# Each query's sum of squares behind its own convolution, and held output rows through the common raw places

## The chip, the cores and the metric

The kernel runs on one core of a Trainium2 chip. Its engines work side by side: TensorE multiplies matrices (PE in the rows below; its weight loads are listed as PEld), VectorE (DVE) and ScalarE (ACT) work element by element, GpSimd (POOL) does small steps, and SyncE (SP) issues most of the DMA transfers. Each engine takes its own instructions in order; between engines, semaphores hold an instruction back until what it reads is there, or until the memory that it writes is free. The metric is the time of the core in microseconds (us) of device time, less is better. The time before is the median of three runs.

## The reference, cut to what matters

`reference` runs a first block (a state-space layer, feed-forward parts, an attention with shared keys and values) and then a second block of two layers on x, 256 positions by 1024 features, in float32. A layer of the second block is a feed-forward part, a hybrid mixer and another feed-forward part. The change is in the hybrid mixer:

```python
hcat = x @ w_in
qa, ka, va, qkv_b, beta_raw, dt_raw, z, gate_raw = jnp.split(hcat, SPLIT_POINTS, axis=-1)
ya = sliding_window_attention(qa, ka, va, pos_bias, sink) @ w_branch_a
qkv_b = jax.nn.silu(causal_depthwise_conv(qkv_b, conv_w))
qb, kb, vb = jnp.split(qkv_b, (QK_B, 2 * QK_B), axis=-1)          # 8 heads of 128
qb, kb = l2norm(qb), l2norm(kb)                                   # t * rsqrt(sum(t * t) + eps)
o = gated_delta_rule(qb, kb, vb, g, beta)                         # chunks of 128 positions
yb = (norm(o) * dn_norm_g * silu(z)) @ w_branch_b
return (gate_a * ya + gate_b * yb) @ w_out
```

The sums of squares of `l2norm` and the last product, that with `w_out`, are what the two edits touch.

## The kernel before, in words

**Weights.** All weights come from DRAM in units of 128 rows by 1024 columns (512 KB). `unit` (L158) takes a raw place, issues the load on SyncE (L161), and splits the values into a high part `wh`, a cast on ScalarE (L150), and a low part `wl`, a subtract on VectorE (L154, for convolutions halved between VectorE and GpSimd). Every product is made of three matmuls: high by high, high by low, low by high. There are three common raw places (WR = 3). SyncE works its queue in order: a load that waits for a place holds back all behind it.

**The mixer's program.** `weave` (L65) writes TensorE's order down when the program is built: tasks in lanes (one delta-rule head each, the preparation of a half, attention windows) are stepped when a model clock says that their inputs are due, and between them stands fill work, which is the list of weight products: z, the decay inputs, the convolutions of heads 0 to 3 and of heads 4 to 7 (keys, then queries, then values, `conv_half`, L1174), the attention projections, z again, the gates, and branch a. `yield hop()` in a task means that it comes back a fixed modelled time later; `yield "name"` means that it waits until fill or another task has put the name into `c.done`. The other engines' instructions are ordered by a scheduler. Branch b (the product with `w_branch_b`) follows the woven part, and behind it comes `w_out`.

**The sums of squares.** `conv` (L1144) computes one head's queries, keys or values: 24 matmuls, a scaled copy on ScalarE, three taps on VectorE, a Tanh, and a last product on VectorE into `kq[m]`, which holds query and key of head m. The preparation of a half, `prep(f)` (L1306), waits for the name `kq{f}`, set when all four queries of the half are there; squares them on ScalarE (line L1314, in four instructions), and adds the squares up with the small matrices `sel` on TensorE into one bank, a row per head. Behind that come a logarithm, the running sum of the decays, a row write by SyncE into DRAM, and loads of these rows by GpSimd, then chunk matrices (one set per head, called `keep2` products of queries and keys, with VectorE masks behind them) and a solve of the small diagonal blocks on GpSimd, whose result is loaded as `T16` and first used in `head` (L1413).

**The end of a head.** ScalarE squares the head's output (L1517), GpSimd makes the inverse root (L1518, L1519), VectorE multiplies (a line of `stt`), TensorE transposes and the result is split. Branch b needs it from all eight heads.

**The held rows.** `row_gemm` (L288) runs the product with `w_out`, eight units of 128 rows. The first three are multiplied as they come. The last five (MH = 5) are loaded and split into a pool of their own and are then gone through four times by `last_rows` (L276), once for each quarter of the output, so that each quarter's layernorm can start early. `hold_pools` (L138) makes the pool, and, where a number of raw places is given (MR = 2), two raw places that only held units use. The first units of the feed-forward part that follows are loaded in the same time.

Of the kernel before, what the change touches and what calls it, by code (L numbers as in the profile page):

```python
# [11 lines left out]
AF = mybir.ActivationFunctionType  # L12
# [4 lines left out]
T = 256  # L17
# [476 lines left out]
TAIL = 3.9  # L494
LAG = 7
HOLD = 6
MH, MR = 5, 2
TS = 8
NC = T // TS
NG, GC, NP = 64, 16, 64  # L500
# [545 lines left out]
NHH = NH // 2  # L1046
# [21 lines left out]
def hybrid(c, i, hT, state, place):  # L1068

    nc, I = c.nc, c.I  # L1070
    V, S, G, PE = nc.vector, nc.scalar, nc.gpsimd, c.pe
# [7 lines left out]
    hop = lambda n=1: n * (HM2 if late else HM)  # L1079
    with ExitStack() as ctx:  # L1080
# [4 lines left out]
        def tile_(kind, *sh, part=P):  # L1085
            n = int(np.prod(sh))
            names = "abcd"[:len(sh)]
            t = pools[kind].tile([P, 512 if kind[-1] == "2" else 256], F32, name=kind)[:part, :n]
            return t.rearrange(f"p ({' '.join(names)}) -> p {' '.join(names)}", **dict(zip(names, sh)))

        k2 = lambda *sh, part=P: tile_("k2", *sh, part=part)
# [11 lines left out]
        sel, cut, msk, lev, bd = c.mixer_consts  # L1103
# [13 lines left out]
        kq, bv, LA, zs, qa, ka, ca, gb, oT, kf, T16, vT = ({} for _ in range(12))  # L1117
# [26 lines left out]
        def conv(f, n, m):  # L1144

            src = n * NH + m
            w = c.unit(W("qkv")[src], SH_C)
            p = c.ps(T)
            yield from c.cols_steps(p, w, hx)
            a = k1(T)  # L1150
            S.activation(out=a, in_=p, func=AF.Copy, scale=cw[:, 3, src:src + 1])
            for d in (1, 2, 3):
                stt(a[:, d:], p[:, :T - d], cw[:, 3 - d, src:src + 1], a[:, d:], ALU.mult, ALU.add)
            h = k1(T)
            c.act(out=h, in_=a, func=AF.Tanh, scale=0.5)
            if n == 2:
                stt(h, h, 1.0, a, ALU.add, ALU.mult)
                return h
            if n == 1:
                kq[m] = keep2(2, T)  # L1160
            stt(kq[m][:, 1 - n], h, 1.0, a, ALU.add, ALU.mult)

        def v_flip(m):
            yield f"vT{m}"
# [9 lines left out]
        def conv_half(f):  # L1174
            heads = range(f * NHH, f * NHH + NHH)
            for n in (1, 0):
                for m in heads:
                    yield from conv(f, n, m)
            c.done.add(f"kq{f}")
            if f == 0:  # L1180
                beta_cols()
            for m in heads:
                vT[m] = yield from conv(f, 2, m)
                c.done.add(f"vT{m}")
# [120 lines left out]

        def prep(f):  # L1306

            yield f"kq{f}"

            pss = c.ps(2, T)  # L1310
            sq = []
            for h in range(NHH):
                sq.append(k2(2, T))
                S.activation(out=sq[h], in_=kq[f * NHH + h], func=AF.Square)  # L1314
            yield hop()
            for h in range(NHH):
                PE.matmul(pss[:NHH], lhsT=sel[:, h, :], rhs=sq[h], start=h == 0, stop=h == NHH - 1)
                yield 0.4
            lr = k2(2, T, part=NHH)
            V.tensor_scalar(out=lr, in0=pss[:NHH], scalar1=4e-6, scalar2=None, op0=ALU.add)  # L1320
            log = c.act(out=lr, in_=lr, func=AF.Ln)
# [39 lines left out]
            for h in range(NHH):  # L1361
                m = f * NHH + h
# [35 lines left out]
            for j in range(15):  # L1398
                n, w = 15 - j, j + 1
# [13 lines left out]
        def head(f, h):  # L1413
# [112 lines left out]
            for t in range(2):  # L1526
# [4 lines left out]

        weave(c,
              [[prep(0)] * (n == 0) + [head(m // NHH, m % NHH) for m in range(n, NH, LH)] for n in range(LH)] +
              [
               [v_flip(m) for m in range(NH)],
# [58 lines left out]
@with_exitstack  # L1594
def build(ctx, tc, I, O, stages):
    c = Core(ctx, tc, I, O)
    nc = tc.nc
    if MAN:
        ctx.enter_context(tc.manual_schedule(engines={mybir.EngineType.PE}))

    c.weight_pools(ctx, WR, WP - 1)
    hT = swish = None
    if "ssm" in stages:
        yT = c.pair(0)
        swish = Glu(c, yT)
        ssm(c, yT, [swish.ahead()])
    c.x = x = c.pool(ctx, "x", 1).tile([P, 2, D], F32, name="x")
    for t in range(2):
        nc.sync.dma_start(out=x[:, t], in_=I["x"][t * P:(t + 1) * P])
    c.hp.append(c.pool(ctx, "h1", 1))  # L1610
    second = "second" in stages or "mix" in stages or "sw" in stages
    if second:
        c.aside = mixer_inputs(c, c.pool(ctx, "mixc", 1))
        if "ffn0" not in stages:
            list(c.aside)


    plan = []
    for i in range(2):
        ffn = lambda j, i=i: ([I["ffn_w13_2_0"][i, j // 2, s] for s in range(2)], "ffn", i, j)  # L1620
        plan += [ffn(0), ([I["w_in_2_z"][i, n] for n in range(2)], "mix", i, 1), ffn(2)]
    plan = plan if "second" in stages else plan[1:3] if "mix" in stages else plan[:1] if "sw" in stages else []

    def ahead(n, hT):
        return c.ahead(hT, plan[n][0]) if n < len(plan) else ([], iter(()))

    with ExitStack() as cn:
        c.norm_pools(cn)
        c.taps = c.pool(cn, "taps", 1)
        hT, state = first_block(c, swish, stages, lambda hT: ahead(0, hT))  # L1630
        if hT is None:
            hT = c.pair(0)
            c.done = {"in0", "in1"}
            for t in range(2):
                c.flip(hT, x[:, t, :], t)
            state, go = ahead(0, hT)
            weave(c, [], [go], drain=True)
    place = 0

    for n, (_, kind, i, j) in enumerate(plan):  # L1640
        if kind == "mix":
            cT = hybrid(c, i, hT, state, 1 - place)
        else:
            place = 1 - place
        with ExitStack() as cn:
            if kind == "mix":
                c.spare_pool(cn)
                c.hold_pools(cn, MH, MR)
            c.norm_pools(cn)
            g, b = c.gains(I["ln_g_2"][i, j]), c.gains(I["ln_b_2"][i, j])  # L1650
            nc.gpsimd.tensor_scalar(out=x, in0=x, scalar1=ALPHA, scalar2=0.0, op0=ALU.mult, op1=ALU.add)
            ho = c.pair(place)
            next_state, go = ahead(n + 1, ho)

            def tail(t, acc):
                if t == 0:
                    c.done -= {"in0", "in1"}
                c.ln(t, acc, 0.5, g, b)
                if n + 1 == len(plan):
                    nc.sync.dma_start(out=O["out"][t * P:(t + 1) * P], in_=x[:, t])  # L1660
                    return
                yield from c.arrive(ho, x[:, t, :], t)

            if kind == "mix":
                weave(c, [], [c.row_gemm(I["w_out_2"][i], c.ktiles(cT), tail, MH), go], drain=True)
            else:
                c.ffn(hT, state, I["ffn_w13_2"][i, j // 2], I["ffn_w2_2"][i, j // 2], c.silu_gate, tail, [go])
        hT, state = ho, next_state
    if not plan:
        nc.sync.dma_start(out=O["out"].rearrange("(t p) d -> p t d", p=P), in_=x)  # L1670
# [218 lines left out]
```

## Time and profile before

| quantity | value |
|---|---|
| time, median of three runs | 2226.42 us (2223.49 to 2230.21) |
| profiled execution, its own time | 2223.28 us |
| span of the profiled execution | 2221.5 us |
| mean granted clock of TensorE | 0.982 of full speed |
| TensorE busy | 2135.0 us, 13908 matmuls |
| VectorE busy | 1537.0 us |
| ScalarE busy | 1182.5 us |
| GpSimd busy | 226.9 us |

The span goes from the first to the last instruction of the profiled execution. The busy shares are means over the whole program; where an engine stands still is read from the waits and the timelines. The two hybrid mixers lie at about 900 to 1280 us and 1650 to 2020 us.

### The profile page before, as it was taken

What the parts mean: (1) busy time and instruction counts of PE and PEld (TensorE: products, weight loads), DVE (VectorE), ACT (ScalarE), POOL (GpSimd) and SP (SyncE); (2) the same over time, 40 slices, a digit from 0 to 9 for tenths busy, and PEclk for the clock granted to TensorE, in tenths of its full rate; (3) what the DMA queues carried; (4) which work ended last, traced back from release to release, by engine and by line L of the source; (5) the groups of instructions that cost most, each with busy time, mean ns of one, the idle gap of its engine ahead of it and who ended that gap; (6) DMA issues with size and microseconds to landing.
All of it is one profiled execution on the core that took longest, in us unless ns stands there. A gap on an engine that the chain in (4) does not pass through costs nothing.

```text
span 2221.5 us, 36550 instructions
## 1 busy us (share of the span) xinstructions
PE 2135.0 (96%) x13908; PEld 1867.4 (84%) x13908; DVE 1537.0 (69%) x2615; ACT 1182.5 (53%) x2187; POOL 226.9 (10%) x360
## 2 busy tenths in 40 slices
PE   8889999999999999998999899999999899998998
PEld 7677888898888888897889788888889788997886
DVE  8855767576877666787755676676678876576665
ACT  4644656444655555465655355545546555544553
POOL 1001000000000000243400000000005242000000
PEclk9889999999999999999999999999999999999999
DMA  4325576543666565554434545555655453264663
GB/s 143 101 35 175 182 247 198 163 124 125 199 189 203 177 189 188 170 173 147 131 105 134 208 152 189 189 191 189 190 171 169 137 167 111 95 206 153 190 190 123
DMA packets 123471, 362.02 MB, mean 163 GB/s; under 512 B 24732, under 2 KB 38000, under 8 KB 123296
## 3 DMA queue, kind: packets, MB, share of 16 engines
q1 hardware_dynamic: 117696, 350.25, 50.4%
q0 software_dynamic: 5232, 9.37, 1.5%
q8 instruction: 110, 1.80, 0.3%
q14 instruction: 65, 0.53, 0.1%
q10 hardware_dynamic: 368, 0.07, 0.0%
HBM read 355.36 MB, written 5.04 MB: 162 GB/s over the span
## 4 chain that ended last, share of the span: by engine, by line
PE 74%; DVE 8%; DMA 7%; issue 4%; ACT 3%; POOL 1%; POOLq 0%; SPq 0%; DVEq 0%; ACTq 0%
PE ps L36 71%; PE ps L40 3%; DVE wl L154 3%; ACT wh L150 2%; DMA raw<-in_w_out_dram 2%; DMA raw<-in_ffn_w_dram 1%; DMA raw<-in_ffn_w_down_dram 1%; DMA raw<-in_w_in_z_dram 1%; DMA raw<-in_ssm_w_glu_dram 1%; DVE keep L1075 1%; DMA k<-scratch 1%; DVE prod L530 1%; POOL k L1074 0%; DVE k L1075 0%; DMA raw<-in_kv_w_v_dram 0%
## 5 line engine op out<-in xcount | busy, mean ns | idle before, releaser
L36 PE MATMUL ps<-xx,wh 128*128 128x256 f32 (+1 forms) x4064 | 1077.4, 340 | 4.6 <-DVE xx L154 2.6
L154 DVE TENSOR_TENSOR wl<-raw,wh 128x1024 fp32r<-128x1024 f32 (+1 forms) x614 | 738.1, 1204 | 332.5 <-ACT wh L150 322.7
L150 ACT CAST wh<-raw 128x1024 fp32r<-128x1024 f32 x614 | 643.6, 1050 | 324.7 <-PE ps L36 171.0
L36 PE MATMUL ps<-xx,wl 128*128 128x256 f32 x2992 | 803.4, 282 | 0.6 <-DVE wl L154 0.6
L36 PEld LDWEIGHTS ps<-xx,wh 128*128 128x128 f32 x4064 | 686.4, 191 | 91.9 <-issue 18.9
L36 PEld LDWEIGHTS ps<-xx,wl 128*128 128x128 f32 x2992 | 568.4, 190 | 22.0 <-DVE wl L154 0.8
L36 PE MATMUL ps<-wh,xx 128*128 128x256 f32 (+1 forms) x1152 | 258.3, 318 | 0.8 <-DVE xx L154 0.7
L225 ACT COPY sum<-ps 128x256 f32<-128x256 f32 x240 | 88.7, 371 | 251.7 <-PE ps L36 251.6
L36 PE MATMUL ps<-wl,gh 128*128 128x512 f32 x528 | 208.6, 395 | 0.0
L36 PE MATMUL ps<-wh,gl 128*128 128x512 f32 x528 | 207.9, 394 | 0.7 <-DVE gl L154 0.7
L36 PE MATMUL ps<-wl,xx 128*128 128x256 f32 (+1 forms) x576 | 189.7, 329 | 19.3 <-DVE wl L154 18.7
L36 PE MATMUL ps<-wh,gh 128*128 128x512 f32 x528 | 207.5, 393 | 0.0
L36 PEld LDWEIGHTS ps<-wh,xx 128*128 128x128 f32 x1152 | 193.5, 193 | 16.5 <-DVE xx L154 3.0
L226 DVE TENSOR_TENSOR sum<-ps,sum 128x256 f32<-128x256 f32 x240 | 101.2, 423 | 112.1 <-ACT sum L225 112.1
L36 PEld LDWEIGHTS ps<-wl,xx 128*128 128x128 f32 x576 | 111.0, 193 | 31.9 <-DVE wl L154 22.6
L36 PEld LDWEIGHTS ps<-wh,gl 128*128 128x128 f32 x528 | 99.0, 188 | 24.7 <-DVE gl L154 1.6
L36 PEld LDWEIGHTS ps<-wh,gh 128*128 128x128 f32 x528 | 99.2, 188 | 22.6
L36 PEld LDWEIGHTS ps<-wl,gh 128*128 128x128 f32 x528 | 99.2, 188 | 18.9 <-ACT gh L150 0.3
L332 POOL TENSOR_SCALAR v<-mv 128x1 f32<-128x1 f32 x12 | 7.3, 609 | 858.2 <-DVE mv L388 858.2
L150 ACT CAST xx<-ps 128x512 fp32r<-128x512 f32 (+1 forms) x64 | 31.8, 512 | 116.3 <-PE ps L40 115.8
L154 POOL TENSOR_TENSOR wl<-raw,wh 128x512 fp32r<-128x512 f32 x48 | 76.7, 1604 | 70.1 <-ACT wh L150 63.1
L1075 DVE SCALAR_TENSOR_TENSOR k<-ps,cw,k 128x255 f32<-128x255 f32 x144 | 68.5, 475 | 2.2
(291 smaller groups left out, 2315.3 us busy)
## 6 DMA issues: line engine op xcount, KB each, us to landing
raw<-in_ffn_w_dram SPq DMA_DIRECT2D x264, 512.0 KB, 3.6
raw<-in_ffn_w_up_dram SPq DMA_DIRECT2D x88, 512.0 KB, 4.2
raw<-in_w_in_qkv_dram SPq DMA_DIRECT2D x48, 512.0 KB, 4.0
raw<-in_ffn_w_down_dram SPq DMA_DIRECT2D x44, 512.0 KB, 3.9
raw<-in_w_in_gate_dram SPq DMA_DIRECT2D x32, 512.0 KB, 3.5
raw<-in_w_branch_dram SPq DMA_DIRECT2D x32, 512.0 KB, 3.5
raw<-in_ssm_w_glu_dram SPq DMA_DIRECT2D x16, 512.0 KB, 3.5
raw<-in_w_in_z_dram SPq DMA_DIRECT2D x16, 512.0 KB, 3.8
```

What stands on the lines that cost most here:

```text
L36: self.pe.matmul(out, lhsT=lhsT, rhs=rhs, start=start, stop=stop)
L40: self.pe.transpose(out, in_, ident)
L150: o = [self.nc.scalar.copy(out=h, in_=src).ins]
L154: r = e.tensor_tensor(out=l[..., c], in0=src[..., c], in1=h.bitcast(F32)[..., c], op=ALU.subtract)
L225: self.nc.scalar.copy(out=s, in_=ps[:, 1])
L226: self.nc.vector.tensor_tensor(out=s, in0=ps[:, 0], in1=s, op=ALU.add)
L332: nc.gpsimd.tensor_scalar(out=v, in0=ms, scalar1=scale, scalar2=eps, op0=ALU.mult, op1=ALU.add)
L530: e.tensor_tensor(out=o, in0=a, in1=b, op=op)
L1075: stt = lambda o, a, s, b, op0, op1, e=V: e.scalar_tensor_tensor(out=o, in0=a, scalar=s, in1=b, op0=op0, op1=op1)
```

## The change

`conv` now puts a name into `c.done` for each query, `prep` waits for one query after the other, squares it, and adds it into the bank when its square is due, and the name for all four is gone. `MR` is gone: held units of `w_out` are loaded into the three common raw places.

```diff
@@ conv
             stt(kq[m][:, 1 - n], h, 1.0, a, ALU.add, ALU.mult)
+            if n == 0:
+                c.done.add(f"q{m}")
@@ conv_half
-            c.done.add(f"kq{f}")
@@ prep
-            yield f"kq{f}"
-
-            pss = c.ps(2, T)
-            sq = []
+
+            pss = None
             for h in range(NHH):
-                sq.append(k2(2, T))
-                S.activation(out=sq[h], in_=kq[f * NHH + h], func=AF.Square)
-            yield hop()
-            for h in range(NHH):
-                PE.matmul(pss[:NHH], lhsT=sel[:, h, :], rhs=sq[h], start=h == 0, stop=h == NHH - 1)
-                yield 0.4
+                yield f"q{f * NHH + h}"
+                yield hop()
+                sq = k2(2, T)
+                S.activation(out=sq, in_=kq[f * NHH + h], func=AF.Square)
+                yield hop()
+                if h == 0:
+                    pss = c.ps(2, T)
+                PE.matmul(pss[:NHH], lhsT=sel[:, h, :], rhs=sq, start=h == 0, stop=h == NHH - 1)
+            yield 0.8
@@ block of the second kind
-MH, MR = 5, 2
+MH = 5
...
-                c.hold_pools(cn, MH, MR)
+                c.hold_pools(cn, MH)
```

TensorE's program in the first mixer, from the last query convolutions of heads 4 to 7 on. Products of `xx` with `wh` and `wl` are a convolution's, those of a square `k2` with `sel` are the sums, those of `keep2` with nothing else named are the first half's chunk matrices. Before:

```order
L36 MATMUL ps_10231<-keep2_9354 128x256 x2
L36 MATMUL ps_10173<-k2_10174,sel_2274 4x512
L36 MATMUL ps_10212<-xx_7255,wh_10207 128x256 x2
...
L36 MATMUL ps_10272<-xx_7255,wl_10268 128x256
L36 MATMUL ps_10173<-k2_10176,sel_2274 4x512
L36 MATMUL ps_10283<-keep2_9395 128x256 x2
L36 MATMUL ps_10173<-k2_10178,sel_2274 4x512
L40 MATMUL ps_10353<-ident_67,k1_9694 128x128 x2
...
L36 MATMUL ps_10272<-xx_7255,wl_10268 128x256
L36 MATMUL ps_10173<-k2_10180,sel_2274 4x512
```

After:

```order
L36 MATMUL ps_10103<-xx_7255,wl_10099 128x256
L36 MATMUL ps_10113<-k2_10035,sel_2274 4x512
L36 MATMUL ps_10103<-xx_7255,wh_10098 128x256 x2
...
L40 MATMUL ps_10238<-ident_67,k2_9983 128x4 x4
L36 MATMUL ps_10113<-k2_10164,sel_2274 4x512
L36 MATMUL ps_10227<-xx_7255,wh_10222 128x256 x2
...
L36 MATMUL ps_10368<-keep2_9313 128x256 x2
L36 MATMUL ps_10113<-k2_10324,sel_2274 4x512
L36 MATMUL ps_10349<-xx_7255,wh_10345 128x256 x2
```

The sums of heads 4 to 7 stood within 22 rows of one another, among the first half's chunk matrices; now they stand 42 to 51 rows apart, and the first of those chunk matrices comes only ahead of the third sum.

TensorE's program at the handover to branch b. The transposes of `k1` with `ident` are those of the last head, whose result branch b reads; products with `xx` are branch a's. Before:

```order
L36 MATMUL ps_12968<-xx_9105,wl_12965 128x256
L40 MATMUL ps_12978<-ident_67,k1_12907 128x128 x2
L36 MATMUL ps_12968<-xx_9105,wh_12964 128x256 x2
...
L36 MATMUL ps_13006<-xx_9105,wl_13003 128x256
L36 MATMUL ps_13039<-keep2_11702,wh_13035 128x256 x2
```

After:

```order
L36 MATMUL ps_12912<-k2_12874,keep2_11065 128x128
L36 MATMUL ps_12977<-xx_9105,wh_12973 128x256 x2
...
L36 MATMUL ps_12977<-xx_9105,wl_12974 128x256
L40 MATMUL ps_13020<-ident_67,k1_12988 128x128 x2
L40 MATMUL ps_13026<-ident_67,k1_13013 128x128 x2
L36 MATMUL ps_13039<-keep2_11913,wh_13035 128x256 x2
```

The last transposes stood 39 matmuls ahead of branch b's first product; now they stand directly ahead of it, and 15 matmuls of branch a lie between the last head's last output product and them.

SyncE's loads at the end of the first mixer; the names end in the weight that is loaded. Before:

```order
L161 DMA raw_13033<-in_w_branch_2_dram 128x1024
L161 DMA raw_13398<-in_w_out_2_dram 128x1024
L161 DMA raw_13404<-in_w_out_2_dram 128x1024
L161 DMA raw_13068<-in_w_branch_2_dram 128x1024
...
L161 DMA raw_13380<-in_w_out_2_dram 128x1024
L161 DMA raw_13428<-in_ffn_w13_2_0_dram 128x1024
...
L161 DMA raw_13410<-in_w_out_2_dram 128x1024
L161 DMA raw_13416<-in_w_out_2_dram 128x1024
...
L161 DMA raw_13422<-in_w_out_2_dram 128x1024
```

After:

```order
L161 DMA raw_13278<-in_w_branch_2_dram 128x1024
L161 DMA raw_13341<-in_w_out_2_dram 128x1024
L161 DMA raw_13359<-in_w_out_2_dram 128x1024
L161 DMA raw_13377<-in_w_out_2_dram 128x1024
L161 DMA raw_13395<-in_w_out_2_dram 128x1024
L161 DMA raw_13401<-in_w_out_2_dram 128x1024
L161 DMA raw_13407<-in_w_out_2_dram 128x1024
L161 DMA raw_13413<-in_w_out_2_dram 128x1024
L161 DMA raw_13419<-in_w_out_2_dram 128x1024
L161 DMA raw_13425<-in_ffn_w13_2_0_dram 128x1024
```

Two held loads stood far ahead, three behind loads of the feed-forward part; now all eight loads of `w_out` stand in a row between the last branch load and the first feed-forward load.

## Rows read from the trace of the kernel before

**Rows 1.** The page: busy us of each engine, share of the span, instructions

```profile
PE 2135.0 (96%) x13908; PEld 1867.4 (84%) x13908; DVE 1537.0 (69%) x2615; ACT 1182.5 (53%) x2187; POOL 226.9 (10%) x360
```

**Rows 2.** PE's waits, whole span: us in total, times, longest us

```profile
PE ps L36 <- DVE wl L154: 19.4, 6, 4.4
PE ps L36 <- ACT k L1314: 11.0, 6, 4.5
...
PE ps L36 <- DVE keep L1074: 2.2, 2, 1.1
```

**Rows 3.** Timeline of PE, first mixer's second squares: start, us, instruction, idle before

```profile
1014.23 1.87 PE L36 MATMUL ps<-k,sel 128*4 128x512 f32 x2 [4.53 <-ACT k L1314]
1016.03 0.80 PE L36 MATMUL ps<-xx,wh 128*128 128x256 f32 x2
...
1019.39 1.02 PE L36 MATMUL ps<-k,sel 128*4 128x512 f32 x2
```

**Rows 4.** Timeline of PE, second mixer's second squares

```profile
1756.41 1.87 PE L36 MATMUL ps<-k,sel 128*4 128x512 f32 x2 [4.53 <-ACT k L1314]
```

**Rows 5.** Timeline of all engines, ahead of the Square in the first mixer

```profile
1012.09 0.42 ACT L274 ACTIVATE k<-k 128x256 f32<-128x256 f32 x1 [3.48 <-DVE k L1075]
...
1013.55 0.63 ACT L1314 ACTIVATE k<-keep 128x512 f32<-128x512 f32 x1 [0.68 <-DVE keep L1075]
```

**Rows 6.** Windows: us; PE, PEld, DVE, ACT, POOL busy; PEclk, DMA, GB/s

```profile
1014.00:1016.00 2.00, 1.77 (x2) 0.09 (x2) 1.90 (x6) 1.01 (x4) 0.00 (x0) 0.50 0.24 96
```

**Rows 7.** Timeline of PE, held output rows of the first mixer

```profile
1256.90 0.40 PE L36 MATMUL ps<-wl,xx 128*128 128x512 f32 x1
...
1257.60 0.39 PE L36 MATMUL ps<-wl,xx 128*128 128x512 f32 x1
...
1262.88 0.79 PE L36 MATMUL ps<-wl,xx 128*128 128x512 f32 x1 [4.43 <-DVE wl L154]
...
1268.69 0.80 PE L36 MATMUL ps<-wl,xx 128*128 128x512 f32 x1 [2.87 <-DVE wl L154]
...
1272.27 0.39 PE L36 MATMUL ps<-wl,xx 128*128 128x512 f32 x1
```

**Rows 8.** Timeline of PE, held output rows of the second mixer

```profile
2000.62 0.39 PE L36 MATMUL ps<-wl,xx 128*128 128x512 f32 x1
...
2016.48 0.40 PE L36 MATMUL ps<-wl,xx 128*128 128x512 f32 x1
```

**Rows 9.** Timeline of SyncE's queue, end of the first mixer

```profile
1213.55 0.81 SPq L161 DMA_DIRECT2D raw<-in_w_out_dram  x2
...
1242.53 9.85 SPq L161 DMA_DIRECT2D raw<-in_ffn_w_dram  x5
...
1254.72 1.46 SPq L161 DMA_DIRECT2D raw<-in_w_out_dram  x2
```

**Rows 10.** Timeline of all engines, splits of the held units, first mixer

```profile
1250.81 1.22 DVE L154 TENSOR_TENSOR wl<-raw,wh 128x1024 fp32r<-128x1024 f32 x1
...
1252.39 3.04 ACT L150 CAST wh<-raw 128x1024 fp32r<-128x1024 f32 x3 [1.06 <-DVE xx L154]
...
1260.53 1.04 ACT L150 CAST wh<-raw 128x1024 fp32r<-128x1024 f32 x1 [2.37 <-DMA raw<-in_w_out_dram]
```

**Rows 11.** DMA issues: how many, KB each, median us from issue to landing

```profile
raw<-in_w_out_dram SPq DMA_DIRECT2D x16, 512.0 KB, 4.2
...
T<-scratch POOLq DMA_DIRECT2D x8, 64.0 KB, 4.4
```

**Rows 12.** Timeline of all engines, the end of a head

```profile
1213.13 0.38 PE L36 MATMUL ps<-k,keep 128*128 128x128 f32 x2
...
1215.29 0.61 DVE L1075 SCALAR_TENSOR_TENSOR k<-ps,ss,keep 128x128 f32<-128x128 f32 x2 [0.86 <-POOL ss L1519]
```

**Rows 13.** Timeline of all engines, the solved blocks' load and first use

```profile
1066.04 1.81 POOL L1409 DMA_DIRECT2D T<-scratch  x2 [2.96 <-DMA scratch<-k]
...
1074.60 0.43 DVE L1074 TENSOR_TENSOR k<-T,blocks 128x256 f32<-128x256 f32 x1
```

## The prediction

> **What bounds the kernel now.** I read the page first. TensorE (PE) is busy for 96% of the span, VectorE (DVE) for 69% [rows 1]. So time can be won only where PE stands still or runs slowly. The view of PE's waits over the whole span says where that is: its largest entry is the wait of products for a weight's low part (19.4 us in 6 times), the second the wait of the sums of squares for ScalarE's (ACT) Square (11.0 us in 6) [rows 2]. The two edits touch exactly these lines. Then I read PE's timeline around both places in both hybrid mixers.
>
> At the squares of heads 4 to 7 (first mixer), the first sum's two matmuls, at 1014.23, had waited 4.53 us for ACT [rows 3]. The second mixer shows the same 4.53 us [rows 4]. Around this stall DVE's end is what ACT waits for: a Tanh waited 3.48 us for a convolution tap that DVE finished late, and the Square at 1013.55 came only behind it, after 0.68 us more of waiting for DVE [rows 5]. In other words, four squares at once wait for the fourth query, and DVE is just then loaded with the first half's chunk matrices. The stall costs more than its length: TensorE's granted clock is 0.50 right behind it, which is the lower of its two levels [rows 6].
>
> At the held output rows (the five last units of w_out), PE stood 4.43 us and again 2.87 us for a low part, and a single product behind each of these waits took 0.79 or 0.80 us instead of 0.40 [rows 7]. SyncE's timeline gives the reason: three of the five held loads stand behind five loads of the feed-forward part that follows, two of them issued at 1254.72, though common raw places were given to those loads from 1242.53 on [rows 9]. ACT's cast of 1260.53 had waited for its load, not for an engine [rows 10].
>
> **Edit 2, held rows through the common places.** It removes the pool of two held raw places. SyncE now issues all eight loads of w_out in a row behind the sixteen branch loads, as the order shows, and the feed-forward loads follow. What was lost: three matmuls of a held unit start 0.69 us apart at full clock (1256.90 to 1257.60 is 0.70). From 1257.60 the third unit's first product was due at 1258.29, and five groups on (3.45 us) the same place is 1261.74, but the row stands at 1272.27: 10.5 us lost [rows 7]. In the second mixer the product due behind 2000.62 at 2001.31 is six groups before the one at 2016.48; 2001.31 + 6 x 0.69 = 2005.45, so 11.0 us are lost [rows 8]. Together 21.5 us. What stays: the held units now take the places that five feed-forward loads had. The last was issued at about 1242.53 + 9.85 - 0.33 = 1252.05 [rows 9]; with 4.2 us to landing [rows 11], 1.04 for the cast [rows 10] and 1.22 for the low part (the subtract of rows 10) its low part is ready at 1258.5. PE asks for the fifth unit's first product four groups behind 1256.90, at 1259.66. The slack is 1.1 us, of the size of one cast in front of it, so I leave 0.5 us a mixer: 20.5 us gained. The bounds are 21.5 (all of it) and 8.8 (rival B). The feed-forward loads, now later, are needed only after the held rows' twenty groups (13.8 us), which covers them.
>
> **Edit 1, one square a query.** The instruction totals stay the same; a query's Square and its two matmuls now stand behind their own query's convolution, about three units apart on PE. What is removed at the second half: the wait of 4.53; two matmuls of a sum at half clock instead of full (1.87 against 1.02 at 1019.39: 0.85 us); and half of the time of the fifteen products at half clock behind them (1016.03 to 1019.39, 3.36: 1.68 us) [rows 3]. That is 7.1 us a mixer, 14.1 for both. The other four waits of the line are 11.0 - 2 x 4.53 = 1.9 us [rows 2, 3, 4] and go too: 16.0.
>
> What is late next? Since the squares no longer bunch up, the first half's sums, its solve and its chunk matrices all move by some 100 rows of PE's program later, onto the last value convolutions and the attention projections, where DVE has less to do. The waits for DVE's products of this kind are 2.2 us in all [rows 2]; I take half as gone, 1.1.
>
> What the edit adds are waits that the trace before does not show. The sum of query 4 stands 33 matmuls (3.7 us at 1.68 for fifteen) behind its convolution, and ahead of its Square on ACT are a cast that waits for PE, a Tanh and a copy; the Square of query 7 stands behind sixteen exponentials. On POOL the second half's four row loads now stand among the first half's solve, behind 2, 3, 6 and 7 of its steps; before, it was 14 and more. The bounds are nothing and the whole present stall, 7.1 a mixer. The nearest rows are the small waits at these lines, 1.9 and 2.2 over both mixers [rows 2], so I take these 4.1 us as coming back in other places.
>
> The order shows one more place, branch b: the last head's transposes stood 39 matmuls ahead of it before, and now directly ahead. The chain that they need is Square on ACT, two steps on POOL and a product on DVE: from the last output product at 1213.13 to the end at 1215.29 + 0.61 it takes 2.77 us [rows 12]. After, only fifteen products (1.68 us) fill that, so 1.1 us are open; with one cast of 1.04 and one low part of 1.22 ahead [rows 10] it is 3.4, and with as much half-clock time behind it as behind the squares (0.85 + 1.68) 5.9. Nothing is the other bound, if PE comes there late for another reason. ACT and DVE have no other deadline there, so I stay near the lower end: 1.5 a mixer, 3.0.
>
> **The sum.** On the profiled execution, 2223.28 us (span 2221.5): -20.5 - 16.0 - 1.1 + 4.1 + 3.0 = -30.5, which makes 2192.8. The median of three runs is 3.1 us above the profiled execution (they lie between 2223.49 and 2230.21), so against the median it is 2195.9: I forecast 2196 us. With everything gained and nothing added (-21.5 - 16.0 - 2.2 = -39.7) it is 2187 by the median, 2184 by the profiled run. With each added wait at its upper end (14.2 + 11.8 in place of 7.1) it is 2215.
>
> **Rival A: the squares' stall is only replaced.** DVE's backlog stays and moves with the chunk matrices; some product waits as long as the Square did. For it: the wait was DVE's, not ACT's [rows 5]. Against it: the first half's matrices now fall on the last two value convolutions and then on the attention projections, which give DVE only a subtract. Then edit 1 is worth nothing, and 2226.4 - 20.5 = 2206.
>
> **Rival B: the held units stay late.** The memory of the held parts may be freed only by the last work of branch b, so that the first wait of 4.43 stays and only the second goes: 2.87, and the 1.5 by which the three groups from 1268.69 to 1272.27 (3.58) are longer than 3 x 0.69. That is 4.4 a mixer, 8.8 instead of 20.5 [rows 7]. For it: the first two held loads, which had places of their own from 1213.55 on, were cast only at the end of branch b (three casts in a row from 1252.39), so something else held them [rows 9, 10]. Against it: by 1252.39 that had ended, and what ACT waits for at 1260.53 is a load [rows 10]. It gives 2195.9 + 11.7 = 2208.
>
> **Rival B2: fewer places, more bubbles.** The same gap twice in a row on PE could say that raw places are short; then taking two away adds a third gap of 5.2 us a mixer (half of 10.5) instead of removing two [rows 7], which is 2226.4 + 10.5 - 10.0 = 2227. Against it: in the time of the gaps, places were being handed to loads that nobody needed yet [rows 9]. The Trainium skill, Perfetto Trace Analysis, section Optimization Strategy, reads a gap that repeats on the engine that should be full as a possible lack of memory for the next tile. By that rule the change should hurt; this trace shows a repeated gap too, but SyncE's rows point at the order of the loads rather than their number, so I give the rule little.
>
> **Rival C, slower: the solve waits in POOL's queue.** The first half's diagonal blocks go through loads that POOL issues: two of them from 1066.04, done issuing 1.81 us later at 1067.85, landing 4.4 us after that [rows 11], at 1072.3, with the first use at 1074.60: 2.3 us of slack [rows 13]. POOL takes its queue in order, and the second half's row loads, each ahead of steps of that solve, wait for a row write by SyncE, which itself stands behind three more weight loads than before and waits with them for raw places. If the write is late by more than 2.3 us, all heads of the first half start late, and what of that isn't covered by fill work comes on PE, in both mixers. To undo the gain and be slower than 2233 it must cost (2233 - 2196) / 2, 18.5 us a mixer. Against it: PE has some hundred rows of gate and attention products to put there.
>
> **How the numbers follow.** Forecast 0.67, A 0.13, B 0.11, B2 0.05, C 0.04. A measurement of this kernel can tell 0.3%, 6.7 us. Forecast, A and B are faster by more: 0.91; B2 is the same: 0.05; C is slower: 0.04. The range from 2183 to 2215 covers the forecast with its bounds, A and B; the forecast's own is 2184 to 2206.
>
> **What would show it.** Right: the entry of 19.4 us in PE's waits falls under 3, that of ACT's Square under 3, and no stretch of granted clock 0.50 is left at either place; SyncE issues the held loads with no feed-forward load among them. The wait at the transposes ahead of branch b is new and about 1 to 3 us. Wrong: a wait for low parts in the held stage of over 4 us (B), a wait for DVE's chunk products of over 3 us around the second half's convolutions (A), a first head's first product that waits for POOL (C).

## The result and the profile after

The changed kernel takes 2203.18 us (median of 4 runs, 2201.46 to 2203.62) against 2228.32 us for the kernel before (4 runs, 2223.49 to 2232.32): a ratio of 0.9892, 95% interval 0.9872 to 0.9911. The medians differ by 25 us (the ratio makes it 24), where 30.5 were forecast. The time lies within the range; of the steps, one failed outright, and one came out near its sum for another reason.

The page of the changed kernel, its span and the busy us of each engine, against [rows 1]:

```profile
span 2201.8 us, 36615 instructions
PE 2125.9 (97%) x13908; PEld 1866.9 (85%) x13908; DVE 1540.2 (70%) x2615; ACT 1181.4 (54%) x2187; POOL 225.5 (10%) x360
```

PE is busy for 9 us less though it runs the same 13908 matmuls. In part that is because fewer of them ran at half clock: the granted clock stood at 0.50 for 70.7 us of the span instead of 79.4. At the squares nothing of this was saved: there it stood at 0.50 for 6.8 us in each mixer in both kernels (in the first mixer from 1012.4 to 1019.1 us before, from 998.0 to 1004.7 now). PE's waits over the span show what is gone and what has come, against [rows 2] (us in total, times, longest us):

```profile
PE ps L40 <- DVE x L393: 18.0, 5, 7.5
...
PE ps L36 <- ACT k L1315: 10.3, 2, 5.4
...
PE ps L36 <- DVE wl L154: 2.6, 2, 2.1
```

The wait for low parts fell from 19.4 to 2.6. The wait for the Square (now line 1315) hardly moved in sum, 11.0 to 10.3, but it is two waits now, one in each mixer. The list of the kernel before has these lines beside [rows 2]:

```profile
PE ps L40 <- DVE x L393: 5.1, 3, 2.0
...
PE ps L40 <- ACT k L274: 2.5, 4, 1.1
...
PE ps L36 <- DVE keep L1075: 1.2, 2, 0.6
PE ps L36 <- DVE k L1075: 1.0, 2, 0.5
PE ps L36 <- ACT k L274: 0.9, 1, 0.9
```

The first is the wait for the last step of a layernorm (line 393); it rose from 5.1 to 18.0. The other four, with the 2.2 us of line 1074 in [rows 2], are small waits in the woven parts of the mixers, for an activation or for a product of VectorE, 7.8 us in all. Of these the changed kernel's list has one line left:

```profile
PE ps L40 <- DVE k L1075: 0.4, 2, 0.2
```

Both kernels run the same 13908 matmuls, and at most places the n-th matmul ends the same stage in both. So the starts of the same matmuls, taken from each trace, cut the time into stages: the woven part from the 5200th to the 7700th matmul, branch b to the 7860th, the output rows with the layernorm behind them to the 8050th; in the second mixer the 10100th, 12560th, 12720th and 12960th. In us, for every kernel run here (the sum of the six is all that the edits touch):

| kernel | woven 1 | b 1 | output 1 | woven 2 | b 2 | output 2 | sum |
|---|---|---|---|---|---|---|---|
| before | 300.0 | 18.1 | 43.9 | 296.8 | 18.4 | 50.1 | 727.3 |
| changed | 295.5 | 18.1 | 39.9 | 289.4 | 18.9 | 48.4 | 710.2 |
| e1 squares alone | 295.0 | 18.1 | 48.2 | 289.4 | 18.9 | 50.5 | 720.1 |
| e2 held rows alone | 299.8 | 18.1 | 39.3 | 297.2 | 18.4 | 45.3 | 718.1 |
| e3 late pair | 295.5 | 18.1 | 36.2 | 290.1 | 18.9 | 42.3 | 701.1 |
| e4 sums later | 310.9 | 19.6 | 40.3 | 298.2 | 25.7 | 46.2 | 740.9 |
| e5 fifth sum later | 293.0 | 18.1 | 40.7 | 290.5 | 18.9 | 47.1 | 708.3 |
| e6 decays four times | 299.1 | 18.1 | 38.5 | 293.3 | 18.9 | 47.4 | 715.3 |
| e7 fifth later, late pair | 289.5 | 18.1 | 35.0 | 287.9 | 19.4 | 40.9 | 690.8 |
| e8 five own places | 295.4 | 18.8 | 35.3 | 289.0 | 18.9 | 41.2 | 698.6 |
| e9 no first hop | 309.2 | 18.1 | 40.3 | 303.4 | 18.4 | 46.6 | 736.0 |
| e10 first half late | 297.6 | 18.1 | 40.3 | 295.3 | 18.9 | 45.6 | 715.8 |
| e11 more on GpSimd | 294.4 | 18.1 | 40.5 | 288.8 | 18.9 | 46.4 | 707.1 |
| e12 decays later | 299.9 | 19.8 | 34.9 | 290.1 | 25.7 | 41.0 | 711.4 |

The two mixers run the same program 4904 matmuls apart, so the places of the second that match those of the first would be the 12604th and the 12764th. In the table "woven 2" stops 44 matmuls short: "b 2" begins with the heads' last transposes, and "output 2" with the end of branch b. At matching places "woven 2" went from 301.6 to 294.6 us, and branch b takes 18.1 us in both mixers, before and after.

The rest of the program, the same code in all, takes between 1474 and 1483 us in these profiles, so single totals scatter by some 9 us, and stages tell more. Of the 17.1 us that the two mixers gained, 11.4 lie in the woven parts and branch b (edit 1), and only 5.7 in the output rows (edit 2), where 20.5 had been forecast.

**Where edit 2's gain went.** SyncE's queue in the first mixer's end, against [rows 9]: the eight loads of w_out stand in a row, as the order said, and the feed-forward loads come behind them, one place after the other until 1260.

```profile
1225.33 17.04 SPq L161 DMA_DIRECT2D raw<-in_w_out_dram  x8
1244.54 2.14 SPq L161 DMA_DIRECT2D raw<-in_ffn_w_dram  x2
...
1248.96 11.20 SPq L161 DMA_DIRECT2D raw<-in_ffn_w_dram  x5
```

PE goes through the twenty held groups without a stop, against [rows 7, 8], and then stands, in the second mixer still longer:

```profile
1258.66 0.62 PE L36 MATMUL ps<-wh,xx 128*128 128x512 f32 x2
1264.08 1.10 PE L40 MATMUL ps<-ident,x 128*128 128x128 f32 x4 [4.79 <-DVE x L393]
...
2001.12 1.11 PE L40 MATMUL ps<-ident,x 128*128 128x128 f32 x4 [7.46 <-DVE x L393]
```

These are the transposes of the first half's normed rows. VectorE's timeline tells why those rows were late:

```profile
1253.49 1.22 DVE L154 TENSOR_TENSOR wl<-raw,wh 128x1024 fp32r<-128x1024 f32 x1 [1.79 <-ACT wh L150]
1254.63 0.68 DVE L385 SCALAR_TENSOR_TENSOR xn<-ps,x 128x512 f32<-128x512 f32 x1
...
1257.32 2.49 DVE L154 TENSOR_TENSOR wl<-raw,wh 128x1024 fp32r<-128x1024 f32 x2 [1.28 <-ACT wh L150]
1259.72 0.68 DVE L385 SCALAR_TENSOR_TENSOR xn<-ps,x 128x512 f32<-128x512 f32 x1
...
1263.28 0.75 DVE L393 SCALAR_TENSOR_TENSOR x<-xn,r,gain 128x512 f32<-128x512 f32 x1 [0.45 <-POOL r L334]
```

The layernorm's first step (line 385, one for each quarter) stands behind two low parts of the next stage's weights, the one of the second quarter behind two more. PE's last held group ends at about 1259.3, so the second quarter was ready ten groups of 0.69 us earlier, at 1252.4; its step started at 1259.72, over 7 us later. VectorE takes its queue in order and waited for the casts, and ScalarE's row shows for what:

```profile
1256.23 1.05 ACT L150 CAST wh<-raw 128x1024 fp32r<-128x1024 f32 x1 [2.78 <-DMA raw<-in_ffn_w_dram]
```

A load that nobody needed yet was late, and what was needed stood behind it. In the kernel before, the same step had all low parts behind it and waited for PE alone; PE's own stalls had given the splits their time:

```profile
1274.53 0.69 DVE L385 SCALAR_TENSOR_TENSOR xn<-ps,x 128x512 f32<-128x512 f32 x1 [2.74 <-PE ps L36]
```

**Where the Square's wait sits now.** In the first mixer it is the fifth query's, against [rows 3]:

```profile
999.62 1.87 PE L36 MATMUL ps<-k,sel 128*4 128x512 f32 x2 [5.40 <-ACT k L1315]
```

Of VectorE's rows, those on the decays of heads 0 to 3 (tiles of 4 partitions) and on that convolution's three taps (a few others, a low part among them, are left out):

```profile
992.40 2.19 DVE L1075 SCALAR_TENSOR_TENSOR k<-k,k 4x256 f32<-4x256 f32 x3
994.52 0.47 DVE L1075 SCALAR_TENSOR_TENSOR k<-ps,cw,k 128x255 f32<-128x255 f32 x1
994.91 1.35 DVE L1074 TENSOR_TENSOR k<-k,k 4x256 f32<-4x256 f32 x1
...
997.00 0.46 DVE L1075 SCALAR_TENSOR_TENSOR k<-ps,cw,k 128x254 f32<-128x254 f32 x1
...
997.72 0.46 DVE L1075 SCALAR_TENSOR_TENSOR k<-ps,cw,k 128x253 f32<-128x253 f32 x1
```

and ScalarE behind it, against [rows 5]:

```profile
998.27 0.42 ACT L274 ACTIVATE k<-k 128x256 f32<-128x256 f32 x1 [4.12 <-DVE k L1075]
...
998.95 1.14 ACT L1315 ACTIVATE k<-keep 128x512 f32<-128x512 f32 x2
```

The three taps of one convolution are spread over 3.7 us with row work of the first half between them. The first half's decays follow its last sum; that sum now comes only 76 matmuls ahead of the fifth query's (the 5690th and the 5766th), so they fall into that query's taps.

### The profile page after: what moved, and what is told of

Its sections match the earlier page's. It is cut to its first block, busy times and chain, and to the rows that moved or that the text cites. A ratio compares the mean times of both kernels' runs of the same rounds, so it can differ in the third digit from the quotient of the medians.

```text
span 2201.8 us, 36615 instructions
## 1 busy us (share of the span) xinstructions
PE 2125.9 (97%) x13908; PEld 1866.9 (85%) x13908; DVE 1540.2 (70%) x2615; ACT 1181.4 (54%) x2187; POOL 225.5 (10%) x360
## 4 chain that ended last, share of the span: by engine, by line
PE 80%; DMA 7%; DVE 6%; ACT 2%; issue 2%; POOL 0%; POOLq 0%; DVEq 0%; SPq 0%; ACTq 0%
PE ps L36 77%; PE ps L40 3%; DMA raw<-in_ffn_w_dram 3%; DVE wl L154 2%; ACT wh L150 2%; DMA raw<-in_w_out_dram 1%; DMA raw<-in_ffn_w_down_dram 1%; DMA raw<-in_w_in_z_dram 1%; DVE prod L530 0%; DMA raw<-in_kv_w_v_dram 0%; DMA raw<-in_ssm_w_glu_dram 0%; DVE gt L530 0%; DVE k L1075 0%; DVE st L386 0%; DMA raw<-in_attn_w_q_dram 0%
## 5 line engine op out<-in xcount | busy, mean ns | idle before, releaser
L36 PEld LDWEIGHTS ps<-xx,wh 128*128 128x128 f32 x4064 | 686.4, 191 | 91.1 <-issue 18.9
```

The lines of the kernel that those rows point to most:

```text
L36: self.pe.matmul(out, lhsT=lhsT, rhs=rhs, start=start, stop=stop)
```

## The experiments

Each ran beside the kernel before; the ratios are to that. All but e2 and e10 have the changed kernel as their base.

**e1, edit 1 alone.**

```diff
-MH = 5
+MH, MR = 5, 2
-                c.hold_pools(cn, MH)
+                c.hold_pools(cn, MH, MR)
```

> Edit 1 alone: one square a query, held output rows with their two own raw places as before. My theory reads the two traces by stage: at the same matmul, the changed kernel gained 5.0 us in the first mixer and 7.0 us in the second up to branch b, and that is edit 1's whole worth. So about 12 us under the kernel before (ratio 0.9946), PE's wait for the Square's line near the 10.3 us of the changed kernel, the wait for low parts in the held stage still near 19 us. Rival: the squares' gain comes only with edit 2 or is chance between two runs; then the ratio lies above 0.998.

2212.44 us, ratio 0.9948 (0.9930 to 0.9967): as expected. The woven parts are those of the changed kernel (295.0, 289.4), and the small waits are gone as there. The held stage keeps its stall, which is even longer; the output stages take 4.3 and 0.4 us more than in the kernel before, and why is open:

```profile
PE ps L36 <- DVE wl L154: 22.9, 7, 6.5
...
PE ps L36 <- ACT k L1315: 9.8, 2, 4.9
PE ps L40 <- DVE x L393: 5.8, 3, 2.1
```

**e2, edit 2 alone** (the kernel before with `c.hold_pools(cn, MH)`).

> Edit 2 alone: the squares four at once as before, held rows through the common raw places. By stage, the held rows gained 10.5 and 11.0 us but 6.6 and 9.3 were given back at the layernorm right behind, so edit 2 nets about 6 us (ratio 0.9974); PE's wait for the layernorm's last step (5.1 us before, 18.0 after) stands near 18. Rival: the layernorm's wait comes from edit 1's new order, and edit 2 alone gains its full 20 us (ratio 0.991) with that wait near 5.

2212.76 us, ratio 0.9958 (0.9941 to 0.9975). The layernorm's wait is there without edit 1; that rival is out. It gained somewhat more than I expected (4.6 and 4.8 us in the output stages). The small waits of the woven parts are all still there, so it is edit 1 that removed them.

```profile
PE ps L40 <- DVE x L393: 15.6, 5, 4.5
...
PE ps L36 <- ACT k L1314: 10.6, 5, 4.5
```

**e3, the second pair of units behind the layernorm.** `load` takes a number of pairs; `self.part` is (1,) for the output rows of a mixer and empty elsewhere:

```diff
+        early, self.early = self.early, None
-        if self.early:
-            self.early()
-            self.early = None
+        if early:
+            early(*self.part)
...
             self.start(tail(t, acc[2 * t:2 * t + 2]))
+            if early and self.part and t == 0:
+                early()
```

> Both edits, and of the four feed-forward units that are loaded ahead during the held rows, the second pair's loads and splits are written behind the first half's layernorm instead of ahead of the held rows. Theory: on VectorE the layernorm stands behind low parts whose loads are late, since two raw places less let them start later; with two of them moved behind it the wait for the layernorm falls from 18.0 to 5 or less, and some 14 us go: about 2189 us (ratio 0.983). Rival: the layernorm chain itself is that long behind unhindered held rows (it was hidden by the stall before); then its wait stays near 18 and the time near 2203 (0.989). Second rival: the moved pair is late itself, and PE waits for its low parts by about what is won.

2192.07 us, ratio 0.986 (0.9833 to 0.9887): under the changed kernel by 11 us by the medians, 9 by the stages and 7 by the two ratios. The layernorm's wait fell to 7.3 and that for low parts is 3.5, so the moved pair is hardly late. On VectorE the second first step now comes at 1253.45 and the low parts behind it:

```profile
1253.45 0.67 DVE L388 SCALAR_TENSOR_TENSOR xn<-ps,x 128x512 f32<-128x512 f32 x1
...
1256.99 0.75 DVE L396 SCALAR_TENSOR_TENSOR x<-xn,r,gain 128x512 f32<-128x512 f32 x1 [0.45 <-POOL r L337]
...
1258.92 2.35 DVE L155 TENSOR_TENSOR wl<-raw,wh 128x1024 fp32r<-128x1024 f32 x2
```

The chain of the layernorm is thus not what was long; its place in VectorE's queue was. It brought 9.8 of the 14 us that I expected: the first of the two pairs still stands ahead.

**e4, the second half's sums later**: `yield hop(3 if f else 1)` between Square and sum.

> Both edits, and each sum of squares of the second half stands two hops (about 32 rows of PE's program, 5.4 us) later. Theory: the 5.40 and 4.9 us that PE now waits for the fifth query's Square come from VectorE, which does the first half's logarithm, decays and rows in the middle of that query's taps; PE only asks too early. Then this wait goes, with the half clock behind it some 7 us a mixer: about 2189 us (ratio 0.983). Rival: VectorE's backlog then holds PE at another place (a PSUM bank, a product of the chunk matrices, later heads); under 5 us are won.

2237.48 us, ratio 1.007 (1.0046 to 1.0093): slower than before, which neither theory had; the rival's direction is right (later heads), its size isn't. The wait for the Square is gone, but the second half's last sum comes 106 rows later, and its heads end late: new waits stand on transposes, and both the woven parts and branch b grew (branch b to 19.7 us in both mixers at matching places; most of the rest of the 25.7 in the table lies ahead of it).

```profile
PE ps L40 <- DVE k L1074: 8.7, 2, 4.5
...
PE ps L40 <- DVE k L1075: 4.3, 2, 2.2
PE ps L40 <- DVE cols L1356: 3.6, 2, 2.1
```

**e5, only the fifth sum later**: `yield hop(3 if f > h else 1)`.

> Both edits, and only the fifth query's sum of squares stands two hops later (32 rows of PE's program); the sums of the other three follow as soon as their lane lets them (19 to 24 rows later than in the changed kernel, where the run with all four later had 51 to 106). Theory: the wait for the Square is a matter of that one query, whose taps VectorE does around the first half's decays; and what the run with all four later lost came from the second half's heads, which all started late and ended late before branch b. So the wait (10.3 us) goes and the heads lose little: 7 us a mixer, about 2189 (ratio 0.983). Rival: the second half's chain has no slack at all; its last sum is about 3 us later, which then comes as a wait ahead of branch b in both mixers, and half of the gain is left: about 2196 (0.986). Second rival: VectorE's backlog holds PE elsewhere in the convolutions, no gain.

2201.08 us, ratio 0.9901 (0.9876 to 0.9926): no gain to speak of. The Square's wait is 0.3, and two others have taken its place, for an attention window's copy and for the decay columns:

```profile
PE ps L36 <- ACT k L1286: 5.7, 2, 3.1
...
PE ps L40 <- DVE cols L1356: 4.5, 2, 2.5
```

The second rival holds: PE is held elsewhere.

**e6, the decays four times.**

```diff
-            stt(ra[:, 0], lr[:, 0], -0.5, gc, ALU.mult, ALU.subtract)
-            stt(ra[:, 1], lr[:, 1], -0.5, gc, ALU.mult, ALU.add)
+            for _ in range(1 if f else 4):
+                stt(ra[:, 0], lr[:, 0], -0.5, gc, ALU.mult, ALU.subtract)
+                stt(ra[:, 1], lr[:, 1], -0.5, gc, ALU.mult, ALU.add)
```

> Both edits, with two of VectorE's row instructions in the first half's preparation (the two that combine logarithm and decays, about 0.7 us each) done four times instead of once; PE's program is unchanged. If these small steps in the middle of the fifth query's taps are what makes its Square late, the six more instructions (about 4.4 us) lengthen PE's wait for the Square from 5.4 and 4.9 to about 9.5 a mixer, and the time by some 9 to 11 us with the half clock behind it: about 2213 (ratio 0.994). Rival: the wait is set by something else (ScalarE's table loads, GpSimd's halves of the low parts); then it stays near 5 and the time within 3 us of 2203.

2211.48 us, ratio 0.9940 (0.9918 to 0.9961). Six instructions more lengthen the wait by 4.15 us a mixer, and the woven parts by 3.6 and 3.9:

```profile
PE ps L36 <- ACT k L1315: 18.6, 2, 9.4
```

So the decays in that convolution's taps are shown to stand in the Square's way.

**e7, e3 and e5 together.**

> Both edits, the fifth query's sum later, and the second pair of feed-forward units behind the layernorm. If the two mended waits are independent, the gains add: 11 us for the pair (measured) and up to 14 for the sum: about 2178 (ratio 0.977), at least 2184 if the second half's chain gives half back.

2191.63 us in 5 runs (2182.91 to 2195.49), ratio 0.9858 (0.9834 to 0.9881): no better than e3 alone, as e5's result would have it, and not the 2178 to 2184 that I expected. Its one profile, at the lower end of that range, has shorter woven parts (289.5, 287.9), which e5 with the same program there has not; that stays open.

**e8, five own places for the held rows**, on e3: `c.hold_pools(cn, MH, 5)`.

> Both edits with the second pair behind the layernorm, but the held rows get five raw places of their own instead of the common three. It asks if the common places were good for their order or if the lack of places still costs. Order theory: with own places the held loads come early, their splits wait for the end of branch b; about the same as the late pair alone, 2192 (ratio 0.986, within 4 us). Places theory: two places less were what made the loads behind late; with five more the rest of the waits around the layernorm goes, 2186 or less. Third: the five splits come in one burst, and PE waits for low parts again, 5 us or more slower.

2191.44 us, ratio 0.9852 (0.9829 to 0.9874), the same as e3. SyncE issued all five held loads far ahead, between 1215.61 and 1219.1, and it bought nothing:

```profile
1215.61 2.10 SPq L162 DMA_DIRECT2D raw<-in_w_out_dram  x3
1218.22 0.91 SPq L162 DMA_DIRECT2D raw<-in_w_out_dram  x2
```

With the pair behind the layernorm, the number of places is not what counts.

**e9, no wait ahead of each Square**: the first `yield hop()` of the loop in `prep` is left out.

> Both edits, without the modelled wait ahead of each Square: still one square a query, but the first half's sums come about two units of 24 matmuls apart instead of three, so its decays and chunk matrices come some 95 rows of PE's program earlier, among the second half's query convolutions, where they were before the change. Theory: edit 1 gained because it made the first half late, off the convolutions in which VectorE is full; then the gain goes: the mixers' woven parts take near 300 and 297 us again (295 and 289 in the changed kernel), the whole about 2213 (ratio 0.995). Rival: the gain is that no sum waits for four queries; then this kernel is as fast as the changed one or faster, 2200 (0.988).

2226.47 us, ratio 1.0022 (1.0007 to 1.0036): slower than either theory had. Still one square a query, and in the sum all of edit 1's gain is gone, and more: with the first half early again (its last sum is the 5544th matmul, as in the kernel before), the Squares' wait is more than twice as long as in the kernel before.

```profile
PE ps L36 <- ACT k L1314: 25.5, 5, 9.5
...
PE ps L36 <- ACT keep L1191: 9.0, 2, 4.9
```

(Its profile is from the upper end of its runs, 2234.86 us; of the stage table the direction counts.) But the wait that is left out stood in both halves. The fifth query's sum is asked for earlier too, at the 5735th matmul instead of the 5766th, and 18.8 of the 25.5 us stand at that sum. So this run does not single out the lateness of the first half; and the small waits that edit 1 removed are gone here as well.

**e10, four at once, but the first half late**: on e2, `yield 0 if f else 16.0` behind the name `kq{f}`.

> Edit 2 with the squares four at once as before, but the first half's preparation starts 16 modelled us later, so that its sums and chunk matrices stand on PE about where the changed kernel has them. Same question from the other side. Theory (lateness of the first half gains, not one square a query): near the changed kernel, 2203 (ratio 0.989), woven parts about 295 and 290 us. Rival (one square a query gains): near edit 2 alone, 2213 (0.996).

2206.69 us, ratio 0.9928 (0.9909 to 0.9947), between the two theories. Against e2 the woven parts are 2.2 and 1.9 us shorter; edit 1 has 4.5 and 7.4. So the lateness of the first half alone is worth about a third of edit 1. The wait for the Square is 9.1 here, near the changed kernel's; of small waits in the woven parts 4.8 us are left, against 7.8 before and 0.4 in the changed kernel. How the rest of edit 1's gain divides between the lateness and one square a query, these runs don't show.

**e11, three quarters of the convolutions' low parts on GpSimd**: `SH_C = 768`.

> Both edits, and GpSimd takes three quarters instead of half of each convolution's low part, which takes some 0.3 us a unit off VectorE; PE's program is unchanged. Theory: VectorE is the bound among the convolutions, and the wait for the fifth Square (10.3 us) is its backlog; it falls to 7 or less, the time by 3 to 6 us: 2199 (ratio 0.987). Rival: GpSimd's part, 2.4 us a unit, becomes the late one, and the convolutions wait for it: slower than 2206.

2201.77 us, ratio 0.9909 (0.9890 to 0.9927), not to be told from the changed kernel. The wait is 9.0 instead of 10.3, the woven parts are 1.1 and 0.6 us shorter: the direction of the theory, not its size. A little less work for VectorE everywhere did little for a burst at one place.

**e12, the decays behind the fifth query**, on e3: behind the last sum, `yield 0.8 if f else 4.0`.

> Both edits and the second pair behind the layernorm, and between the first half's last sum and its decays the lane waits 4 modelled us instead of 0.8, so that on VectorE the decays stand behind the fifth query's last product instead of ahead of it; its sum stands where it was on PE, and the first half's chunk matrices come 23 rows later. Theory: the decays in the fifth query's taps are what the Square waits for (four times the decays made that wait 18.6 us in all); out of its way it falls from about 10 us to 3 or less, the woven parts take 290 and 284 us or less, and the whole some 11 us less than the late pair alone: 2181 (ratio 0.981). Rival: VectorE has no room in this stretch, as the run with the fifth sum later showed, and the wait comes back at the next heads or ahead of branch b: 2190 (0.985).

2204.98 us, ratio 0.9922 (0.9907 to 0.9937), 13 us slower than e3 and slower than either theory had. The wait for the Square fell to 1.1, so the cause is shown from this side too; but waits for a Tanh and ahead of branch b came instead, and branch b takes 1.7 and, at matching places, 2.3 us longer:

```profile
PE ps L36 <- ACT k L275: 7.8, 2, 4.0
...
PE ps L40 <- DVE k L1079: 4.3, 2, 2.2
PE ps L36 <- DVE k L1510: 2.4, 2, 1.2
```

The rival is right in what came (the wait came back), and the second half's heads have no slack before branch b. Its reason is not what the trace shows at the Tanh: VectorE had room there, busy for 4.5 of the 10 us from 1005 to 1015. It stood still for a row load of the first half's chunk matrices, and the convolution's last tap stood behind that product in its queue (in the second mixer it stood 5.77 us):

```profile
1013.61 0.69 DVE L1078 TENSOR_TENSOR k<-k,masks 128x512 f32<-128x512 f32 x1 [5.47 <-DMA k<-scratch]
1014.22 0.48 DVE L1079 SCALAR_TENSOR_TENSOR k<-ps,cw,k 128x253 f32<-128x253 f32 x1
```

## Why the prediction was right or wrong

**Held rows: wrong, at the step on the feed-forward loads.** What was lost before (10.5 and 11.0 us) was read rightly, and the wait for low parts went (19.4 to 2.6). The step that failed is "the feed-forward loads, now later, are needed only after the held rows' twenty groups, which covers them". PE did not need them earlier. But their low parts stood on VectorE ahead of the layernorm, which PE does need. Net, the output stages gained 4.0 and 1.7 us instead of 20.5 in all (with edit 2 alone 4.6 and 4.8); e3 shows the cause by moving two of the four low parts.

**Squares: the sum near, the way wrong, and that is luck.** Forecast were -16.0 - 1.1 + 4.1 = -13.0; the woven parts gained 4.5 + 7.4 = 11.9. But I had taken the stall as gone, and it stayed, 10.3 us instead of 11.0, with its 6.8 us at half clock in each mixer. It stands at the fifth query alone, behind the first half's decays (e6, e12), which I had placed with the moved work without looking where in VectorE's program they fall. By its mechanism rival A came true; its price, edit 1 worth nothing, did not. What was gained lies in a term that I had mis-sized. I took the waits for VectorE's products for a side effect, 2.2 us in one row, half of it gone: 1.1. Small waits of this kind and for activations stood in five rows, 7.8 us in all, and 0.4 are left (e1; in e2 they stand as before). The 4.1 us that I let come back in other places did not come. Waits explain some 8 of the gain; the rest is in no row of the waits.

**Branch b: too dear.** I added 3.0 us for the last transposes directly ahead of it; branch b itself took as long as before, the 44 matmuls up to its start in the table, with the last transposes, took 5.7 us instead of 5.2 in each mixer, and the waits at these transposes are 0.4 us in all. A choice near the bound of nothing would have been better; that the place is tight showed only when the heads came later still (e4, e12).

**The rivals.** Of the signs of being right, the wait for low parts (2.6) and SyncE's row of loads came; the Square's wait (10.3) and the transposes' (0.4 instead of 1 to 3) did not. B did not come: held units were on time. B2 did not come as a third gap in the held rows. A lack of places would still fit the late feed-forward loads, but with the pair behind the layernorm five own places changed nothing (e8). The Trainium skill (Perfetto Trace Analysis, Optimization Strategy) reads a repeated gap as a possible lack of memory; here it was the order in the queues, 2191.4 us with five own places against 2192.1 without. C did not come: no wait in the list is for GpSimd's loads.

**The time.** By stages the mixers gained 17.1 us where 30.5 were forecast: 14.8 less at the held rows (5.7 instead of 20.5), and 1.4 more at the squares and branch b together (11.4 instead of 13.0 - 3.0 = 10.0). That the total missed by no more than it did is owed to the squares' small waits, not to the way that was forecast. The profiled spans differ by 19.7 us, and 2.7 of that is code that was not touched (1480.6 us in the profile before, 1477.9 in that after). The medians differ by 25; the rest is scatter of the kernel before, whose runs here lie up to 9 us apart.

## What to carry to other kernels

A load that is put behind others because nobody needs it yet still has its place in the queues of the engines that unpack it: ask what stands behind its cast and its subtract there, not only when the matrix engine wants it. A stall can pay for the next stage's loads, and when it goes, they have to be found another place; here that meant to write two of them behind the layernorm (e3, 2192 us, the best of these kernels together with e7 and e8). And a wait that is moved can come back at the next reader: it did in e4, e5 and e12. In e12 the trace shows why: the next reader's tap stood in VectorE's queue behind a product that waited 5.47 us for a load. So before moving a wait, look at what stands ahead in that queue, and whether the engine works or waits in that time. What would gain at the Square, no run here shows.

## What the runs showed of the hardware

TensorE's granted clock was 0.50 right behind the 5.40 us wait, as behind the 4.53 us before [rows 6]:

```profile
999.00:1003.00 4.00, 3.38 (x9) 1.67 (x10) 3.31 (x8) 1.87 (x5) 1.74 (x3) 0.50 0.80 237
```

What I had not expected is how much the same instructions differ between runs: the first 5200 matmuls, which no kernel here changes, took from 916.1 to 923.6 us in these profiles. In the stretch from 50 to 160 us the granted clock was 0.84 in the profile before and 0.89 in that after:

```profile
50.00:160.00 110.00, 91.42 (x645) 77.06 (x643) 82.62 (x127) 58.12 (x99) 0.00 (x0) 0.89 0.31 70
```

So a few us of a single profile's total can come from code that was not touched.
